# Two decoder layers on one core: first loads in order of use, one reader per PSUM bank, the last feature tile late in its group, and a fixed TensorE order in the last dilated pair

## The chip, the core and the metric

The kernel runs on 1 core of one Trainium2 chip. The metric is the device time of one execution in microseconds; three runs of the kernel before the change gave 2347.19, 2353.07 and 2353.18, so their median is 2353.07. Besides, one execution was profiled, and every row of the profile comes from that one.

## What is computed

One sequence of 512 tokens of width 1024 goes through two layers. Each layer has three sub-layers: a SwiGLU feed-forward (FFN), a token mixer and a second FFN. The mixer of layer 0 is multi-head latent attention (MLA), that of layer 1 is a dilated sliding-window attention with three dilations. Every sub-layer is wrapped in the same way:

```python
def sandwich(x, fn, pre_g, post_g, shift, scale, gate, res_w):
    hn = rmsnorm(x, pre_g) * (1 + scale[:, None, :]) + shift[:, None, :]
    y = rmsnorm(fn(hn), post_g)
    return x + res_w * gate[:, None, :] * y

def swiglu(h, w_gate, w_up, w_down):
    return (jax.nn.silu(h @ w_gate) * (h @ w_up)) @ w_down
```

Shift, scale and gate are products of silu(c) with a large matrix, `w_mod`: 2 x 1024 x 9216. All data is float32.

## The kernel before

**Layout.** Tokens are cut into four tiles of 128 (`TT`), the model width into eight tiles k of 128 (`KT`), the hidden width 2816 of an FFN into 22 feature tiles. The normed and modulated input of a sub-layer is kept transposed in `t.h`, one tile of 128 x 512 for each k.

**Three products for one.** Each float32 operand is split into a high part (`hi`, rounded to the fast matmul type) and a low part (`lo`, the rest). `mm3` (lines 123 to 128) adds hi x hi, hi x lo and lo x hi into one PSUM bank, on lines 125, 126 and 127. So every block of weights is loaded into a raw buffer (`load`, a ring of `RAW` = 5 buffers of 512 KB), copied to `whi` on ScalarE (L108) and subtracted into `wlo` on VectorE (L110). The split weights live in a ring of 6 slots (`weights`), or in general slices of 128 x 512 (`weights_sliced`, L119 and L120), of which there are 44.

**Modulation.** `mod` (L140) loads 512 KB of `w_mod` and reduces it with silu(c) on VectorE (L144). 144 such reductions are needed, 8 for each of the three vectors of each of six sub-layers. 16 are done in `start` (in halves, `mod_load` L152 and `mod_halves` L159, called `fetch` and `fold` there); the other 128 stand in the list `todo`, and `pump(n)` does the next n of them. When the last of a gate vector is done, `mod_out` writes the vector of 1024 to DRAM (`row`, L199), and `gates` reads it back broadcast (L215). `settle` pumps what a sub-layer still lacks when a border comes.

**The start.** `__init__` issues the loads of x and c and computes silu(c) on ScalarE (L71). `start` (L308) squares each token tile and sums it (L284), takes the root on GpSimd (L292), scales the tile on ScalarE (L306), transposes it on TensorE (L333) into eight banks, and then modulates k by k. The first four units (feature tiles of gate and up, `START`) are accumulated over k together, in eight banks.

**Modulating.** `modulate` (L269) makes the high part of `h` on ScalarE from the source (L275). The low part comes from a second pass over the source: on VectorE (L280, L281), or, with `spare`, on ScalarE and GpSimd (L277, L278). At a border, `turn` (L420) does this for 256 tokens with k in `SPARE` on GpSimd; the source is a PSUM bank that holds two k.

**An FFN.** Feature tiles are taken in four groups of 5 or 6 (`GROUPS`). For each, `head` multiplies gate and up (48 matmuls of 512 columns), and `gate_up_out` makes g: SiLU (L478), product (L480), high part (L481), low part (L483). After a group, `down` (L490) multiplies the group's g with its rows of `w_down`, for four token tiles i and two halves d of the width, and `y_part` adds the bank to y. The last group's `down` is `tail`, part of the border. `rest` (L515) holds the loops, and in them the calls of `pump`.

**A border.** `transition` (L390) runs `tail(i)` for the four token tiles, finishes each in `tile_done` (residual and, in `normal`, the next norm), emits `turn` for two tiles after some matmuls, and then the heads of the next sub-layer in two halves of 256 tokens.

**The dilated mixer.** Heads come in eight pairs. For each pair `scores` multiplies q and k and takes maxima, `tops` sends the maxima through DRAM to bring three dilations to one order (L1002 to L1022), `exps` does the exponentials on ScalarE (L1037), and `mix` transposes them (L1086) and multiplies with v (L1111). `Mixer.part` is the product of the first three pairs' outputs with the output weights, which is independent of the last pairs; `put_o` splits a pair's output (L599, L600).

**Order.** The framework plans the order of instructions on each engine and of the loads on SyncE's queue (SP) from the order of the program, priorities and its own estimate of when things are ready; on the chip each engine then works strictly in that order.

Of the kernel before, what the change touches and what calls it, by code (L numbers as in the profile page):

```python
# [11 lines left out]
PSUM = bass.MemoryType.PSUM  # L12

# [11 lines left out]
PUMP = 1  # L25
# [7 lines left out]
SPARE = (1, 3, 5, 7)  # L33
# [19 lines left out]
class Trunk:  # L53
    def __init__(self, ctx, tc, a):
# [16 lines left out]
        nc.scalar.activation(self.cs, self.cs, AF.Silu)  # L71
# [197 lines left out]
    def modulate(self, sub, k, lo, hi, src, spare=False):  # L269

        nc = self.nc
        a, b = self.scale(sub, k)
        u = self.t("u", UB)[:, : hi - lo]
        hh, hl = [x[k][:, lo:hi] for x in self.h]
        nc.scalar.activation(hh, src, AF.Identity, bias=b, scale=a)  # L275
        if spare:
            nc.scalar.activation(u, src, AF.Identity, bias=b, scale=a)  # L277
            nc.gpsimd.tensor_tensor(hl, u, f(hh), ALU.subtract)  # L278
        else:
            nc.vector.tensor_scalar(u, src, a, b, ALU.mult, ALU.add)  # L280
            nc.vector.tensor_tensor(hl, u, f(hh), ALU.subtract)  # L281
# [15 lines left out]

    def normal(self, i, out):

        nc = self.nc  # L300
        ss = self.pair()
        for d in range(2):
            self.square(self.x[:, i, d * SEQ : (d + 1) * SEQ], out[d], ss[:, d : d + 1])
        r = self.scale_of(ss)
        for d in range(2):
            nc.scalar.activation(out[d], self.x[:, i, d * SEQ : (d + 1) * SEQ], AF.Copy, scale=r)  # L306

    def start(self, sub):  # L308
# [18 lines left out]
        fetch(1)  # L327
        xt = [self.bank("mm" if k < 4 else "aux") for k in range(KT)]
        for i in range(TT):
            t = [self.s(), self.s()]  # L330
            self.normal(i, t)
            for k in range(KT):
                nc.tensor.transpose(  # L333
                    xt[k][:, i * P : (i + 1) * P], t[k // 4][:, k % 4 * P :][:, :P], self.ident
                )
            if i < 2:
                fold(i)
        self.new_h()
        for k in range(2):
            self.modulate(sub, k, 0, SEQ, xt[k])  # L340
        for k in range(2, KT):
            src, xt[k] = xt[k], self.s()
            if k % 2:
                nc.vector.tensor_copy(xt[k], src)
            else:
                nc.scalar.activation(xt[k], src, AF.Copy)
        units = range(START)
        banks = {}
        for u in units:
            banks[u] = [self.bank("mm" if 2 * u + g < 4 else "aux") for g in range(2)]  # L350
        for u in units:
            if u == START - 1:
                fetch(2)
            sub.gate_up_load(u, u >= SLOTS // 2)
            if u == 1:
                feed((0, 1), (0,))
                feed((0, 1), (1,))
            elif u:
                feed((u,), (0, 1))
        fold(2)  # L360
        for k in range(2, KT):
            if k + 1 < KT:
                fetch(k + 1)
            self.modulate(sub, k, 0, SEQ, xt[k])
            if k + 1 < KT:
                fold(k + 1)
            feed(units, (k,))
# [6 lines left out]
    def y_part(self, i, d, b, first):  # L374

        nc = self.nc
        with self.tc.high_priority(offset=HOT):
            y = self.y[i][d]
            if first:
                nc.scalar.activation(y, b, AF.Copy)  # L380
            else:
                nc.vector.tensor_tensor(y, b, y, ALU.add)  # L382
# [7 lines left out]
    def transition(self, sub, nxt):  # L390
# [45 lines left out]
class Ffn:  # L436
# [14 lines left out]

    def gate_up_mm(self, ft, lo, hi, banks, ks):
# [37 lines left out]
    def down(self, q, i, d):  # L490
# [8 lines left out]
        b = t.bank()  # L499
        for j in range(m):  # L500
            t.mm3(
                b,
                [x[j][:, i * P : (i + 1) * P] for x in self.g[q]],
                [x[:, d * SEQ : (d + 1) * SEQ] for x in self.wd[q][j]],
# [775 lines left out]
```

## Time and profile before

| | |
|---|---|
| three runs | 2347.19, 2353.07, 2353.18 us |
| profiled execution | 2343.64 us |
| its span | 2341.8 us |
| matmuls recorded | 11418 |
| TensorE clock granted, mean | 0.992 |
| moved by DMA | 284.55 MB, 122 GB/s in the mean |

In a row of the timeline stand the start and the duration in us, the engine, the line, the operation, what it writes and reads, how many are merged and, in brackets, how long the engine was idle before it and what released it. A row of the list of waits has the total in us, the number and the longest. A row of a window has its width, the busy time of the engines (with counts), TensorE's clock, the DMA engines' share and GB/s; where only TensorE was asked for, one busy time stands there. PE is TensorE, DVE VectorE, ACT ScalarE, POOL GpSimd, SP the queue of loads.

### The profile page before, as it was taken

What the parts mean: (1) busy time and instruction counts of PE and PEld (TensorE: products, weight loads), DVE (VectorE), ACT (ScalarE), POOL (GpSimd) and SP (SyncE); (2) the same over time, 40 slices, a digit from 0 to 9 for tenths busy, and PEclk for the clock granted to TensorE, in tenths of its full rate; (3) what the DMA queues carried; (4) which work ended last, traced back from release to release, by engine and by line L of the source; (5) the groups of instructions that cost most, each with busy time, mean ns of one, the idle gap of its engine ahead of it and who ended that gap; (6) DMA issues with size and microseconds to landing.
All of it is one profiled execution on the core that took longest, in us unless ns stands there. A gap on an engine that the chain in (4) does not pass through costs nothing. (4 is left out here: it accounts for less than half of the span.)

```text
span 2341.8 us, 30216 instructions
## 1 busy us (share of the span) xinstructions
PE 2259.5 (96%) x11418; PEld 1858.3 (79%) x11418; DVE 1182.7 (51%) x2647; ACT 890.0 (38%) x1791; POOL 116.7 (5%) x160
## 2 busy tenths in 40 slices
PE   6999999999999999999999999999999899999998
PEld 4888787877788788887888888778777668888887
DVE  6666655577564465465454453434443446333344
ACT  4332135577543132362222253443434246332222
POOL 0000001210110000030000020000000002000000
PEclk9999999999999999999999999999999999999999
DMA  8567641211264364245643523333333322233230
GB/s 307 178 211 232 206 153 62 92 55 55 67 199 140 116 198 144 72 128 170 179 140 119 163 81 102 85 94 86 89 82 90 94 54 81 91 117 99 81 108 36
DMA packets 119925, 284.55 MB, mean 122 GB/s; under 512 B 43985, under 2 KB 48356, under 8 KB 119780
## 3 DMA queue, kind: packets, MB, share of 16 engines
q1 hardware_dynamic: 119780, 282.63, 39.0%
q8 instruction: 89, 1.46, 0.2%
q14 instruction: 56, 0.46, 0.1%
HBM read 280.19 MB, written 2.39 MB: 121 GB/s over the span
## 5 line engine op out<-in xcount | busy, mean ns | idle before, releaser
L125 PE MATMUL mm<-s,whi 128*128 128x512 f32 (+1 forms) x2292 | 850.4, 373 | 8.5 <-ACT s L275 4.3
L126 PE MATMUL mm<-s,whi 128*128 128x512 f32 (+1 forms) x2292 | 846.4, 370 | 12.0 <-POOL s L278 9.8
L127 PE MATMUL mm<-s,wlo 128*128 128x512 f32 (+1 forms) x2292 | 845.1, 369 | 4.2 <-DVE wlo L110 4.2
L108 ACT ACTIVATE whi<-raw 128x1024 fp32r<-128x1024 f32 (+1 forms) x366 | 380.6, 1053 | 1016.6 <-PE mm L126 475.3
L110 DVE TENSOR_TENSOR wlo<-raw,whi 128x512 fp32r<-128x512 f32 (+1 forms) x732 | 479.2, 693 | 430.6 <-ACT whi L108 425.4
L125 PEld LDWEIGHTS mm<-s,whi 128*128 128x128 f32 x2292 | 433.4, 190 | 93.8 <-issue 7.0
L126 PEld LDWEIGHTS mm<-s,whi 128*128 128x128 f32 x2292 | 434.7, 190 | 85.4 <-POOL s L278 13.3
L127 PEld LDWEIGHTS mm<-s,wlo 128*128 128x128 f32 x2292 | 434.7, 190 | 77.2 <-DVE wlo L110 5.5
L125 PE MATMUL mm<-whi,s 128*128 128x512 f32 x848 | 333.3, 393 | 8.8 <-ACT s L481 8.7
L127 PE MATMUL mm<-whi,s 128*128 128x512 f32 x848 | 330.8, 391 | 3.5 <-DVE s L483 3.4
L126 PE MATMUL mm<-wlo,s 128*128 128x512 f32 x848 | 330.5, 390 | 0.0
L144 DVE CUSTOM_DVE_ANT_0 raw<-raw,cs 128x1024 f32<-128x1024 f32 x128 | 156.9, 1228 | 116.8 <-DMA raw<-w_mod 116.3
L125 PEld LDWEIGHTS mm<-whi,s 128*128 128x128 f32 x848 | 159.5, 188 | 45.4 <-ACT s L481 11.3
L127 PEld LDWEIGHTS mm<-whi,s 128*128 128x128 f32 x848 | 159.3, 188 | 40.2 <-DVE s L483 6.6
L126 PEld LDWEIGHTS mm<-wlo,s 128*128 128x128 f32 x848 | 159.6, 188 | 32.5 <-issue 0.2
L382 DVE TENSOR_TENSOR s<-mm,s 128x512 f32<-128x512 f32 x112 | 77.1, 689 | 163.1 <-PE mm L127 163.0
L480 DVE TENSOR_TENSOR gg<-silu,mm 128x512 f32<-128x512 f32 (+1 forms) x95 | 60.4, 636 | 161.1 <-PE mm L127 155.6
L292 POOL TENSOR_TENSOR mv<-mv,mhalf 128x1 f32<-128x1 f32 x48 | 38.1, 794 | 1590.6 <-DVE mv L291 1590.6
L481 ACT ACTIVATE s<-gg 128x512 fp32r<-128x512 f32 (+1 forms) x97 | 57.4, 592 | 62.7 <-DVE gg L480 59.4
L380 ACT ACTIVATE s<-mm 128x512 f32<-128x512 f32 x48 | 28.0, 593 | 84.2 <-PE mm L127 84.2
L1037 ACT ACTIVATE u<-u,y 128x128 f32<-128x128 f32 x128 | 49.5, 388 | 27.4 <-DVE y L1018 27.4
L937 ACT ACTIVATE s<-mm 128x512 f32<-128x512 f32 (+3 forms) x156 | 46.3, 374 | 30.7 <-PE mm L127 30.7
(159 smaller groups left out, 1485.1 us busy)
## 6 DMA issues: line engine op xcount, KB each, us to landing
raw<-w_gu SPq DMA_DIRECT2D x176, 512.0 KB, 4.6
raw<-w_mod SPq DMA_DIRECT2D x128, 512.0 KB, 4.6
raw<-w_down SPq DMA_DIRECT2D x88, 512.0 KB, 3.7
raw<-dil_in SPq DMA_DIRECT2D x72, 512.0 KB, 3.6
s<-w_mod SPq DMA_DIRECT2D x32, 256.0 KB, 6.3
raw<-mla_o SPq DMA_DIRECT2D x8, 512.0 KB, 3.5
raw<-dil_o SPq DMA_DIRECT2D x8, 512.0 KB, 4.4
gb<-row SPq DMA_DIRECT2D x6, 512.0 KB, 4.8
```

Of the source, the lines that this page charges most:

```text
L108: self.nc.scalar.activation(hi, raw, AF.Copy)
L110: self.nc.vector.tensor_tensor(lo[:, r], raw[:, r], f(hi[:, r]), ALU.subtract)
L125: mm(out, w[0], m[0], start=first, stop=False)
L126: mm(out, w[0], m[1], start=False, stop=False)
L127: mm(out, w[1], m[0], start=False, stop=last)
L144: nc.vector.tensor_tensor_reduce(raw, raw, self.cs, 1.0, 0.0, ALU.mult, ALU.add, accum_out=t[:, 0:1])
L292: nc.gpsimd.tensor_tensor(v[:, 1:2], v[:, 0:1], self.mhalf[:, 0:1], ALU.pow)
L382: nc.vector.tensor_tensor(y, b, y, ALU.add)
L480: nc.vector.tensor_tensor(v, s, banks[1], ALU.mult)
L481: nc.scalar.activation(ghi, v, AF.Copy)
L937: nc.scalar.activation(out, src, AF.Copy)
L1037: nc.scalar.activation(c, c, AF.Exp, bias=pair["top"][:, g, i, one], scale=-1.0, accum_out=pair["z"][:, g, i, one],)
```

## The change

1. Loads of the start: silu(c) moves behind the squares of x on ScalarE; the scalings go to VectorE; the work by k and by unit is interleaved (k=0, unit 0, k=1, unit 1, ...), and loads on SP keep the order of the program there.
2. `modulate` without `spare` reads its source once, on VectorE, and ScalarE makes the high part from that copy; with `spare` ScalarE alone reads it. `SPARE` becomes (2, 3, 6, 7), so that both k of a bank have the same reader. `normal` scales one half on VectorE.
3. `down` runs both halves d of token tile 0 without the last feature tile, then that one.
4. Reductions are pumped in gate and up alone: three for a unit in the first FFN, two in the others; none in `down`.
5. `prepare` loads and splits the next sub-layer's first weights into slices behind token tile 1 of a border.
6. Last dilated pair: three outputs are split and the first output weights loaded earlier, the parts' copies go to VectorE, and TensorE keeps the program's order through the parts and the mixing steps.

```diff
-PUMP = 1
-SPARE = (1, 3, 5, 7)
+SPARE = (2, 3, 6, 7)
...
         nc.sync.dma_start(self.cs, a["c"].broadcast_to([P, D]))
-        nc.scalar.activation(self.cs, self.cs, AF.Silu)
...
         hh, hl = [x[k][:, lo:hi] for x in self.h]
-        nc.scalar.activation(hh, src, AF.Identity, bias=b, scale=a)
         if spare:
+            nc.scalar.activation(hh, src, AF.Identity, bias=b, scale=a)
             nc.scalar.activation(u, src, AF.Identity, bias=b, scale=a)
             nc.gpsimd.tensor_tensor(hl, u, f(hh), ALU.subtract)
         else:
             nc.vector.tensor_scalar(u, src, a, b, ALU.mult, ALU.add)
+            nc.scalar.activation(hh, u, AF.Copy)
             nc.vector.tensor_tensor(hl, u, f(hh), ALU.subtract)
...
-        for d in range(2):
-            nc.scalar.activation(out[d], self.x[:, i, d * SEQ : (d + 1) * SEQ], AF.Copy, scale=r)
+        self.nc.scalar.activation(out[0], x[0], AF.Copy, scale=r)
+        self.nc.vector.tensor_scalar(out[1], x[1], r, None, ALU.mult)
...
         fetch(0)
-        fetch(1)
         xt = [self.bank("mm" if k < 4 else "aux") for k in range(KT)]
+        with self.tc.manual_schedule(engines={ACT, DVE}):
+            for i in range(TT):
+                t, ss, x = [self.s(), self.s()], self.pair(), self.halves(i)
+                for d in range(2):
+                    self.square(x[d], t[d], ss[:, d : d + 1])
+                r = self.scale_of(ss)
+                for d in range(2):
+                    nc.vector.tensor_scalar(t[d], x[d], r, None, ALU.mult)
+                for k in range(KT):
+                    nc.tensor.transpose(
+                        xt[k][:, i * P : (i + 1) * P], t[k // 4][:, k % 4 * P :][:, :P], self.ident
+                    )
+            nc.scalar.activation(self.cs, self.cs, AF.Silu)
         self.new_h()
...
+        for kind, n in sorted([(n, 1) for n in range(START)] + [(n, 0) for n in range(KT)]):
+            kind, n = n, kind
+            if kind:
+                sub.gate_up_load(n, n >= SLOTS // 2)
+                banks[n] = [self.bank("mm" if 2 * n + g < 4 else "aux") for g in range(2)]
+                units.append(n)
+                feed((n,), ks)
+                continue
+            if n:
+                fetch(n)
+            fold(n)
+            self.modulate(sub, n, 0, SEQ, xt[n], n in (3, 5, 7))
+            ks.append(n)
+            feed(units, (n,))
+            if n == 0:
+                for k in range(1, KT):
+                    src, xt[k] = xt[k], self.s()
+                    nc.scalar.activation(xt[k], src, AF.Copy)
...
-    def y_part(self, i, d, b, first):
+    def y_part(self, i, d, b, first, busy=False):
...
+            if not first:
+                nc.vector.tensor_tensor(y, b, y, ALU.add)
+            elif busy:
+                nc.vector.tensor_copy(y, b)
+            else:
                 nc.scalar.activation(y, b, AF.Copy)
...
                 self.after(TURN, lambda i=i: self.turn(nxt, i - 1))
+            if nxt and i == 1:
+                nxt.prepare()
...
+    def prepare(self):
+        self.gate_up_load(0, True)
...
+        b = [None, None]
+        for js in (range(m - 1), (m - 1,)) if i == 0 else (range(m),):
+            for d in range(2):
+                b[d] = b[d] or t.bank()
+                self.products(b[d], q, i, d, js)
+                if m - 1 in js:
+                    t.y_part(i, d, b[d], q == 0)
+                    if q == len(GROUPS) - 1:
+                        t.y_done(i, d)
...
                 self.head(ft, 0, SEQ)
-                t.pump(PUMP)
+                t.pump(3 if t.first is self else 2)
             for i in range(TT if q < last else 0):
-                for d in range(2):
-                    self.down(q, i, d)
-                    if t.first is self:
-                        t.pump(2 - d)
-                    elif d or q == 0:
-                        t.pump(1)
+                self.down(q, i)
...
+    def prepare(self):
+        self.w = {u: self.t.weights_sliced(self.t.a["mla_in"][u]) for u in range(2)}
...
+                if (c, i) == (7, 0):
+                    self.t.new_y()
...
+    def prepare(self):
+        t = self.t
+        self.wt = {(0, u): t.weights_sliced(t.a["dil_in"][0, u]) for u in self.ORDER[:2]}
...
         self.scores(7, 1)
+        for x in self.of[:PART]:
+            self.put_o(x)
         self.mix(6, 3)
+        t.new_y()
+        for j in range(PART):
+            self.out_weights(j)
         self.scores(7, 2)
         self.mix(6, 4)
         self.scores(7, 3)
-        for x in self.of:
+        for x in self.of[PART:]:
             self.put_o(x)
         self.exps(7)
-        for n in range(6):
-            self.part(n)
-        for step in range(5):
-            self.mix(7, step)
-            if step in (1, 2):
-                self.part(5 + step)
+        with t.tc.manual_schedule(engines={PE}):
+            for n in range(6):
+                self.part(n)
+            for step in range(5):
+                self.mix(7, step)
+                if step in (1, 2):
+                    self.part(5 + step)
         self.put_o(self.of[-1])
...
-        t.start(first)
+        with tc.manual_schedule(engines={SP}):
+            t.start(first)
```

More of the change, by code (lines that the diff above doesn't have):

```diff
@@ L12 @@
 PSUM = bass.MemoryType.PSUM
+PE, ACT, DVE, SP = (getattr(mybir.EngineType, n) for n in ("PE", "Activation", "DVE", "SP"))
 P = 128
@@ L296, in pair, with halves @@
         return self.tmp.tile([P, 2], F32, tag="ss", name="ss", bufs=6)
+    def halves(self, i):
+        return [self.x[:, i, d * SEQ : (d + 1) * SEQ] for d in range(2)]
     def normal(self, i, out):
-        nc = self.nc
-        ss = self.pair()
+        ss, x = self.pair(), self.halves(i)
         for d in range(2):
-            self.square(self.x[:, i, d * SEQ : (d + 1) * SEQ], out[d], ss[:, d : d + 1])
+            self.square(x[d], out[d], ss[:, d : d + 1])
         r = self.scale_of(ss)
-        for d in range(2):
-            nc.scalar.activation(out[d], self.x[:, i, d * SEQ : (d + 1) * SEQ], AF.Copy, scale=r)
+        self.nc.scalar.activation(out[0], x[0], AF.Copy, scale=r)
+        self.nc.vector.tensor_scalar(out[1], x[1], r, None, ALU.mult)
     def start(self, sub):
@@ L326, in start @@
         fetch(0)
-        fetch(1)
         xt = [self.bank("mm" if k < 4 else "aux") for k in range(KT)]
[L329 to L337, printed above, removed]
-        self.new_h()
-        for k in range(2):
-            self.modulate(sub, k, 0, SEQ, xt[k])
@@ L341, in start @@
[L341 to L347, printed above, removed]
-        banks = {}
[L349 to L367, printed above, removed]
+        with self.tc.manual_schedule(engines={ACT, DVE}):
[11 more added lines that the diff above has]
+            nc.scalar.activation(self.cs, self.cs, AF.Silu)
@@ L488, in head, with products, down @@
         self.gate_up_out(ft, lo, hi, banks)
-    def down(self, q, i, d):
+    def products(self, b, q, i, d, js):
+        m = GROUPS[q][1]
+        for j in js:
+            self.t.mm3(
+                b,
+                [x[j][:, i * P : (i + 1) * P] for x in self.g[q]],
+                [x[:, d * SEQ : (d + 1) * SEQ] for x in self.wd[q][j]],
+                j == 0,
+                j == m - 1,
+            )
+    def down(self, q, i):
         t = self.t
@@ L498, in down @@
                 t.new_y()
[L499 to L504, printed above, removed]
-                j == 0,
-                j == m - 1,
-            )
-        t.y_part(i, d, b, q == 0)
+        b = [None, None]
[7 more added lines that the diff above has]
+                        t.y_done(i, d)
     def tail(self, i):
-        for d in range(2):
-            self.down(len(GROUPS) - 1, i, d)
-            self.t.y_done(i, d)
+        self.down(len(GROUPS) - 1, i)
     def rest(self):
@@ L557, in __init__, with out_weights @@
         self.o = [[], []]
+    def out_weights(self, j):
+        t = self.t
+        if j not in self.wo:
+            self.wo[j] = t.weights(t.a[self.w_o][j], flat=True)
     def products(self, b, i, d, js):
@@ L574, in part @@
         i, d = divmod(n, 2)
-        if n == 0:
-            self.t.new_y()
         b = self.t.bank()
         self.products(b, i, d, range(PART))
-        self.t.y_part(i, d, b, True)
+        self.t.y_part(i, d, b, True, self.busy)
     def tail(self, i):
@@ L606 @@
     heads = 6
+    busy = False
     w_o = "mla_o"
@@ L613, in head @@
             if u == 0:
-                self.w, self.lat, self.sq = {}, {}, {}
+                self.lat, self.sq = {}, {}
                 self.latn = {}
@@ L618, in head @@
                     nc.sync.dma_start(x, t.a["mla_tab"][q])
-            self.w[u] = t.weights(t.a["mla_in"][u])
+            if u not in self.w:
+                self.w[u] = t.weights(t.a["mla_in"][u])
             self.lat[u] = t.s()
@@ L832 @@
     heads = 6
+    busy = True
     w_o = "dil_o"
```

13 lines of the change are left out of this document (5 added, 8 removed).

## The prediction

> **What bounds the kernel now.** I read the page first, then the list of who waited for whom on PE, then windows over the stages, then the timeline of each place that the list names.
>
> ```profile
> span 2341.8 us, 30216 instructions
> PE 2259.5 (96%) x11418; PEld 1858.3 (79%) x11418; DVE 1182.7 (51%) x2647; ACT 890.0 (38%) x1791; POOL 116.7 (5%) x160
> PE mm L333 <- ACT s L306: 19.5, 4, 17.0
> PE aux L1086 <- ACT sq L1037: 13.8, 5, 7.9
> PE mm L126 <- POOL s L278: 9.8, 12, 2.2
> PE mm L125 <- ACT s L481: 8.7, 5, 3.6
> PE mm L127 <- DVE s L483: 3.4, 4, 1.3
> ```
>
> TensorE is the bound: it is busy for 96% of the span, and the change takes no matmul away. All that can be won lies in the 82 us in which PE is idle, and in slow matmuls behind a stall. The rows (us in total, times, longest) name the places: the start (L333), the softmax of the dilated pairs (L1086), the hidden tiles at a sub-layer's border (L278), and the last feature tile of a group (L481, L483). The profiled execution took 2343.64 us, 1.8 more than its span; the median of the three runs shown is 2353.07, 9.4 above it. Gains are summed against the profiled one.
>
> **The start.** Now: first tokens, then weights.
>
> ```profile
> 9.98 1.06 ACT L71 ACTIVATE cs<-cs 128x1024 f32<-128x1024 f32 x1 [7.97 <-DMA cs<-c]
> 27.56 0.79 PE L125 MATMUL mm<-s,whi 128*128 128x512 f32 x1 [0.22 <-DVE u L280]
> 79.00 0.39 PE L127 MATMUL aux<-s 128*128 128x512 f32 x1
> 79.22 0.39 PE L125 MATMUL mm<-s,whi 128*128 128x512 f32 x1
> x<-x SPq DMA_DIRECT2D x4, 512.0 KB, 4.4
> 16.00:20.00 4.00, 2.20 (x9) 1.80 (x10) 1.71 (x8) 3.56 (x8) 0.71 (x2) 1.00 1.03 410
> 54.17 0.69 DVE L159 CUSTOM_DVE_ANT_0 s<-s,cs 128x512 f32<-128x512 f32 x1
> 57.49 0.15 DVE L189 SCALAR_TENSOR_TENSOR mA<-mt,small 128x1 f32<-128x1 f32 x1
> 33.07 4.30 DVE L110 TENSOR_TENSOR wlo<-raw,whi 128x512 fp32r<-128x512 f32 x7
> L280 DVE TENSOR_SCALAR u<-s,mA,mS 128x512 f32<-128x512 f32 x6 | 3.3, 546 | 0.1
> ```
>
> ACT's first operation is SiLU of c, so the squares of x, which lands earlier, stand behind it until 11. The first four units are 4 x 8 x 6 = 192 matmuls; at 0.227 us apart (79.00 to 79.22) they are 43.5 us, but they run from 27.56 to 79.22, where unit 4 begins: 8.2 us are lost after a late begin.
>
> After the change x goes first, and SP's order is k=0, unit 0, k=1, unit 1, and so on. Up to unit 0 that is 2.1 MB of x, 0.5 of c and 2.1 of weights: 4.7 MB at the 410 GB/s of the window, 11.5 us, some 15 with the launch. From then on each k with its unit is 2.1 MB, 5.1 us. DVE is slower: between 54.17 and 57.49 lie five reductions with their small operations, 0.69 each, so a fold of four is 2.8; a weight half is 4.30/7 = 0.61, a unit 2.5; modulating is 0.55 + 0.61 = 1.2. That is 6.5 us per k and unit. From about 12, when the folds can begin, DVE has k=0 and unit 0 at 19, then 25.5, 32, 37 (k=3 is modulated on ACT and POOL), and the last k near 51. PE has 6, 18, 30, 42 and four times 24 matmuls in these steps. With the first 24 at the half pace shown below it ends at 33, 40, 49.5 and 71.3. **Gain 7.5 us.** Bounds: if PE ran without a break from 18 it would end at 61.5 (gain 17.7); if the half pace and DVE's steps lasted longer, nothing is gained. The subtraction of a whole k on POOL has no row here (256 columns take 0.72, below), so 0.7 to 3.6; PE's backlog of 5.4 us per k hides it. Two orders become fixed. On ACT, SiLU of c stands behind all squares, and DVE's folds wait for it; it is 1.06 us, and ends near 12, before the first modulation weights matter to PE. On SP, the sixth 512 KB load (the second half of unit 2) waits for one of five buffers, which unit 0's split frees by 19, and the loads of k=3 stand behind it; DVE wants them at 32, so the 13 us between cover the wait and four loads of 0.65.
>
> **The last feature tile of a group.** Down products of token tile 0 need g of a unit that has just ended.
>
> ```profile
> 1074.99 1.23 DVE L144 CUSTOM_DVE_ANT_0 raw<-raw,cs 128x1024 f32<-128x1024 f32 x1 [3.09 <-DMA raw<-w_mod]
> 1076.15 0.68 DVE L480 TENSOR_TENSOR gg<-silu,mm 128x512 f32<-128x512 f32 x1
> 1077.55 0.80 PE L125 MATMUL mm<-whi,s 128*128 128x512 f32 x1 [3.62 <-ACT s L481]
> ```
>
> PE covers 12 or 15 matmuls of d=0 (2.7 or 3.4 us), then stands; here gg stood behind a modulation reduction that waited 3.09 us for its load. The change does both d without the last j first: 24 or 30 matmuls, 5.4 or 6.8 us. The cover grows by 2.7 to 3.4, and no stall of this kind is longer than 3.62. Of 8.7 + 3.4 = 12.1 us some 1 stays. Moving the reductions from down to gate-up (3 a unit in the first FFN, 2 later) puts more of them ahead of gg, so I take **11 us** of bounds 6 to 13 (matmuls right after the longest stall are slow too, as after the one below).
>
> **The sixth dilated pair, by the moved reductions.**
>
> ```profile
> 1850.15 0.38 SPq L199 DMA_DIRECT2D row<-mG  x1
> 1851.72 0.37 SPq L1015 DMA_DIRECT2D x<-m  x1
> 1864.46 0.17 DVE L1017 TENSOR_TENSOR y<-x 128x8 f32<-128x8 f32 x1 [11.52 <-DMA x<-m]
> 1869.43 1.18 PE L1086 MATMUL aux<-ident,sq 128*128 128x128 f32 x3 [7.86 <-ACT sq L1037]
> 1872.40 0.78 PE L125 MATMUL mm<-s,whi 128*128 128x512 f32 x1
> 1875.85 0.39 PE L127 MATMUL mm<-s,wlo 128*128 128x512 f32 x1
> 1910.90 0.17 DVE L1017 TENSOR_TENSOR y<-x 128x8 f32<-128x8 f32 x1 [2.23 <-DMA x<-m]
> row<-mG SPq DMA_DIRECT2D x1, 4.0 KB, 9.1
> ```
>
> The maxima come back 12.7 us after their issue; in the next pair DVE waits 2.23 for the same load. Just ahead of it in the queue stands row<-mG, 4 KB that took 9.1 us at another place, where its landing is shown. That row belongs to the last FFN: 128 reductions remain after the start, and before the change the FFNs pump 54 + 35 + 35, with 2 more at the border behind MLA, so 2 are left for the dilated layer. After it they pump 54 + 2 + 38 + 34, and all are done in the FFN ahead. The row leaves this queue. Then the maxima are in some 9 us earlier and the transposes can begin near 1860, when PE comes to them at 1861.6. Eight transposes follow; the 7.86 and 0.7 us of stall go, and the eight matmuls from 1872.40 to 1875.85, 0.43 apart, run at full pace (1.6). **Gain 11 us**, bounds 0 (another cause) to 11.6. Where the row now goes, an FFN with loads far ahead, a late weight could cost up to those 9; the row of 9.1 lay in an FFN without a stall of PE, so I take nothing.
>
> **The last pair, with PE's order fixed.**
>
> ```profile
> 1900.00:1926.00 26.00, 21.73 (x148) 15.15 (x145) 13.96 (x51) 12.98 (x54) 0.00 (x0) 0.87 0.14 23
> 1915.24 2.06 PE L1086 MATMUL aux<-ident,sq 128*128 128x128 f32 x6 [4.04 <-ACT sq L1037]
> 1921.12 0.38 ACT L1037 ACTIVATE u<-u,y 128x128 f32<-128x128 f32 x1
> ```
>
> PE runs four parts, then stands 4.04 us. The order puts six parts (54 matmuls, 12.2 us) ahead of the transposes and one between each of the next steps. That fills the stall, but ACT's exponentials still end at 1921.5, and in a fixed order PE waits there for tiles that it could pass before. I take **3 us** of bounds -2 to 5. The six copies out of PSUM go to DVE, 0.69 each as any 512-wide operation there: 4.1 more beside 13.96 of 26 us. The early weights and put_o of three tiles only fill idle time; new_y moved in MLA costs nothing.
>
> **The borders.** Five windows, width against PE's busy time:
>
> ```profile
> 399.00:425.00 26.00, 22.20 (x160) 0.93 0.46 162
> 625.00:650.00 25.00, 19.85 (x134) 1.00 0.46 148
> 1000.00:1026.00 26.00, 21.56 (x143) 1.00 0.43 130
> 1380.00:1400.00 20.00, 16.83 (x99) 0.91 0.42 139
> 1960.00:1982.00 22.00, 18.49 (x112) 0.92 0.40 141
> 1015.90 3.61 POOL L292 TENSOR_TENSOR mv<-mv,mhalf 128x1 f32<-128x1 f32 x1 [3.02 <-DVE mv L291]
> 1019.49 0.72 POOL L278 TENSOR_TENSOR s<-u,s 128x256 fp32r<-128x256 f32 x1
> 1016.02 3.09 DVE L110 TENSOR_TENSOR wlo<-raw,whi 128x512 fp32r<-128x512 f32 x5
> ```
>
> Idle: 3.8 + 5.2 + 4.4 + 3.2 + 3.5 = 20.1 us. The change splits the next weights two token tiles early (up to 2 to 4 ACT and 4 DVE operations leave the border), gives DVE one of two scalings in normal, and moves POOL from k=1 to k=2, so that the first two tiles come from DVE. ACT and DVE no longer hand a bank to each other, but hh now waits for u. The count on POOL stays four per turn. I take **8 us** of bounds 0 to 14. POOL's power at 1015.90 took 3.61 us exactly while DVE ran five splits, and the hl behind it held PE 2.2 us. The Trainium skill (SBUF — State Buffer, "Who interferes with whom") says that the pair of ports that DVE and GpSimd share is an exclusive lock, and the loser blocks; the 3.61 agrees. By that rule early splits help here, but two POOL tiles in a row, 2 and 3, double what one blocked operation holds up, and the borders would gain nothing.
>
> **Sum.** 7.5 + 11 + 11 + 3 + 8 = 40.5: 2343.64 - 40.5 = 2303 as profiled, 2312 beside the median.
>
> **Rivals.**
> - *New waits for old* at borders and group ends: POOL's pairs stall behind DVE's runs, and reductions delay gg. Borders 0, groups 6: 13 us less, 2325. For it: 3.61 and 3.09 above. Chance 0.16.
> - *The maxima are late for another cause*, such as the 512 KB load between row and maxima: 2323. Against it: other pairs have such loads too. Chance 0.08.
> - *The start stays at half pace*: PE is fed in bursts of 6 and 12. The 0.43 us above follow a stall of 7.86. The gain of 7.5 goes: 2320. The Trainium skill (TensorE: Matmul & The Clock Gate, "HAM oscillation — how this bites in real kernels") says that waits over some 3.4 us between short bursts send the clock back to half each time. Chance 0.08.
> - *Slower: DVE becomes the bound in the first FFN.*
>
> ```profile
> L144 DVE CUSTOM_DVE_ANT_0 raw<-raw,cs 128x1024 f32<-128x1024 f32 x128 | 156.9, 1228 | 116.8 <-DMA raw<-w_mod 116.3
> ```
>
> A unit is 48 matmuls, 10.9 us. DVE would have 2.5 of splits, 1.3 of g and three reductions of 1.23 with small operations, 4.5: 8.3. The row has 116.3 us of waiting for loads in 128, 0.9 each, 2.7 a unit: 11.0, just the bound. If a unit waited 6 us more, 18 units would lose over 60 with the 40 won: 2370. It decides against the change from 2.4 us a unit on. Against it: those waits fall mostly where DVE has nothing else. Chance 0.05.
> - *Nothing moves*, since the planner had these orders already: 2350. Against it: the orders on SP and PE are forced. Chance 0.03.
>
> **How the numbers follow.** The forecast has 0.60, with a range of its own of 2296 to 2322 (start 0 to 17.7, pair -2 to 5, borders to 14). The range takes in the first three rivals with some spread: 2292 to 2336. About 0.3% (7 us) is what a measurement can tell from no change, so faster means under 2346: 0.88 with the tail of the first rivals left out; within 0.06; slower 0.06.
>
> **What would show it.** PE's first matmul near 19 and unit 4 near 71; no row<-mG in the dilated layer and no wait for x<-m over 3 us; L481 and L483 gone from PE's list; L1086 under 5 us; the five border windows with some 12 us of idle. It is wrong if DVE waits for w_mod in gate-up show behind PE stalls for weight splits, or if POOL's waits grow.

## The result, and the profile after

Four runs of the changed kernel gave 2309.79 to 2314.05 us, median **2313.09**; four of the kernel before in the same group gave 2344.48 to 2353.18, median 2350.13. The ratio is 0.9843, with a 95% interval of [0.9818, 0.9867]. The forecast was 2312. The changed kernel's profiled execution took 2314.05 us, 29.6 less than the 2343.64 of before, where 40.5 had been summed: between the medians lie 37.0, and the profiled execution of before lay below all four runs of its kernel, that of after is the slowest of its four. The sum of the steps is therefore judged against the 29.5 us by which the two profiled spans differ, the stages against each other. One run of the kernel before, in the last group of experiments, took 6388.67 us and is left out everywhere.

The page, first part, of the kernel after:

```profile
span 2312.3 us, 30176 instructions
...
PE 2247.3 (97%) x11418; PEld 1857.3 (80%) x11418; DVE 1191.8 (52%) x2674; ACT 870.6 (38%) x1773; POOL 121.4 (5%) x163
```

The list of what PE waited for, of the kernel after (us in total, times, longest):

```profile
PE mm L124 <- DVE s L378: 16.4, 1, 16.4
PE mm L125 <- POOL s L277: 14.5, 13, 2.2
PE mm L124 <- ACT s L280: 7.6, 4, 6.4
PE mm L339 <- DVE s L337: 7.1, 1, 7.1
PE aux L248 <- POOL rs L242: 2.6, 4, 1.2
PE aux L1107 <- ACT sq L1058: 1.7, 4, 0.9
```

The lines have moved: L339 is the transposes of the start (L333 before), L280 the high part of h, L277 GpSimd's subtraction (L278), L1107 the transposes of a dilated pair (L1086), L378 the copy of a part out of PSUM, which is new on VectorE. Read against the list of before: the start's 19.5 us became 7.1 + 7.0 (of L280's), the group ends (L481 and L483, 12.1) are gone, the pairs' 13.8 became 1.7. Two rows speak against the forecast. GpSimd's wait rose from 9.8 to 14.5, which the prediction had named as a sign of being wrong, and one stall of 16.4 us is new, longer than anything that was removed behind the start.

Stage by stage, from PE's timeline (a border is counted from its first transpose on L427 to its last, a body from one border to the next; the last body ends with the last matmul, and the last dilated pair begins with the first matmul of its parts, at 1902.40 before and 1863.10 after):

| stage | before | after | gain | forecast |
|---|---|---|---|---|
| start, to unit 4 | 79.2 | 71.4 | 7.8 | 7.5 |
| four FFN bodies (the first from unit 4) | 1364.9 | 1345.6 | 19.3 | 11 |
| MLA body | 201.0 | 201.7 | -0.7 | 0 |
| five borders | 134.1 | 130.7 | 3.4 | 8 |
| dilated layer, through pair 6 | 500.3 | 489.7 | 10.6 | 11 |
| its last pair and parts | 54.0 | 64.9 | -10.9 | 3 |

These add up to 29.5.

### The profile page after: what moved, and what is told of

It reads as the page before. It is cut to its first block, busy times and chain, and to the rows that moved or that the text cites. A ratio compares the mean times of both kernels' runs of the same rounds, so it can differ in the third digit from the quotient of the medians.

```text
span 2312.3 us, 30176 instructions
## 1 busy us (share of the span) xinstructions
PE 2247.3 (97%) x11418; PEld 1857.3 (80%) x11418; DVE 1191.8 (52%) x2674; ACT 870.6 (38%) x1773; POOL 121.4 (5%) x163
## 5 line engine op out<-in xcount | busy, mean ns | idle before, releaser
L124 PE MATMUL mm<-s,whi 128*128 128x512 f32 (+1 forms) x2132 | 804.7, 379 | 10.2 <-ACT s L280 7.0
L125 PE MATMUL mm<-s,whi 128*128 128x512 f32 (+1 forms) x2132 | 800.2, 375 | 0.9 <-POOL s L277 0.7
L126 PE MATMUL mm<-s,wlo 128*128 128x512 f32 (+1 forms) x2132 | 799.1, 375 | 0.0
L107 ACT ACTIVATE whi<-raw 128x1024 fp32r<-128x1024 f32 (+1 forms) x356 | 370.2, 1053 | 989.8 <-PE mm L125 447.8
L109 DVE TENSOR_TENSOR wlo<-raw,whi 128x512 fp32r<-128x512 f32 (+1 forms) x712 | 464.9, 692 | 414.2 <-ACT whi L107 409.2
L124 PEld LDWEIGHTS mm<-s,whi 128*128 128x128 f32 x2132 | 403.6, 190 | 92.7 <-ACT s L280 8.2
L125 PEld LDWEIGHTS mm<-s,whi 128*128 128x128 f32 x2132 | 403.9, 189 | 71.7 <-POOL s L277 2.1
L126 PEld LDWEIGHTS mm<-s,wlo 128*128 128x128 f32 x2132 | 403.8, 189 | 71.2
L124 PE MATMUL mm<-whi,s 128*128 128x512 f32 x848 | 333.4, 393 | 17.1 <-DVE s L378 16.4
L483 DVE TENSOR_TENSOR gg<-silu,mm 128x512 f32<-128x512 f32 (+1 forms) x95 | 60.3, 636 | 172.4 <-PE mm L126 172.0
L292 POOL TENSOR_TENSOR mv<-mv,mhalf 128x1 f32<-128x1 f32 x48 | 27.3, 568 | 1492.6 <-DVE mv L291 1492.6
L481 ACT ACTIVATE silu<-mm 128x512 f32<-128x512 f32 (+1 forms) x95 | 51.6, 544 | 34.0 <-PE mm L126 33.7
L125 PE MATMUL mm<-s 128*128 128x256 f32 x160 | 47.6, 303 | 14.8 <-POOL s L277 13.8
```

Of the source, the lines that this page charges most:

```text
L107: self.nc.scalar.activation(hi, raw, AF.Copy)
L109: self.nc.vector.tensor_tensor(lo[:, r], raw[:, r], f(hi[:, r]), ALU.subtract)
L124: mm(out, w[0], m[0], start=first, stop=False)
L125: mm(out, w[0], m[1], start=False, stop=False)
L126: mm(out, w[1], m[0], start=False, stop=last)
L292: nc.gpsimd.tensor_tensor(v[:, 1:2], v[:, 0:1], self.mhalf[:, 0:1], ALU.pow)
```

## The experiments

Each kernel is the changed one with one edit, unless it says otherwise; times are medians of four runs, beside runs of the kernel before on the same chip. There were four groups: `parts_first` to `down_whole`; `spare_old` to `prepare_off`; the changed kernel again with `silu_first` and `pf_sub`; and `pumps_back`. The kernel before took 2351.9, 2344.8, 2346.4 and 2348.5 us in them, so between groups the ratios are compared. Line numbers shift by one where an edit adds or takes a line.

| kernel | us | ratio to before |
|---|---|---|
| changed kernel, with the result above | 2313.09 | 0.9843 [0.9818, 0.9867] |
| changed kernel, again (third group) | 2312.03 | 0.9855 [0.984, 0.987] |
| `parts_first` | 2300.86 | 0.9786 [0.9765, 0.9808] |
| `free_order` | 2303.65 | 0.9798 [0.9779, 0.9818] |
| `row_back` | 2321.9 | 0.9881 [0.9858, 0.9904] |
| `down_whole` | 2320.79 | 0.987 [0.9848, 0.9892] |
| `spare_old` | 2304.9 | 0.983 [0.9816, 0.9845] |
| `sub_dve` | 2297.58 | 0.9798 [0.9783, 0.9813] |
| `sp_free` | 2319.17 | 0.9893 [0.9876, 0.9909] |
| `prepare_off` | 2315.49 | 0.9876 [0.9859, 0.9893] |
| `silu_first` | 2314.22 | 0.9866 [0.985, 0.9883] |
| `pumps_back` | 2328.3 | 0.991 [0.9894, 0.9927] |
| `pf_sub` (two edits) | 2286.43 | 0.9743 [0.9729, 0.9758] |

### The new stall in the last pair

VectorE's timeline of the kernel after, around the stall:

```profile
1871.44 0.17 DVE L1038 TENSOR_TENSOR y<-x 128x8 f32<-128x8 f32 x1 [2.94 <-DMA x<-m]
...
1886.65 0.17 DVE L1079 TENSOR_TENSOR w<-x 128x8 f32<-128x8 f32 x1 [14.84 <-DMA x<-z]
...
1887.26 2.43 DVE L378 COPY s<-mm 128x512 f32<-128x512 f32 x4
```

L1079 is the denominators of the softmax on their way back from DRAM: they exist only when all exponentials are done, so VectorE stands 14.84 us. The four copies, whose sources PE had finished by 1871.5, lie behind it in the same queue, back to back as soon as it lets go. PE has four banks for parts, all full, and its fixed order forbids it to go on to anything else. In `parts_first` the parts are emitted ahead of the exponentials, so that the copies stand ahead of L1079; in `free_order` the copies stay behind it and PE's order is free.

```diff
 parts_first:
-        self.exps(7)
         with t.tc.manual_schedule(engines={PE}):
             for n in range(6):
                 self.part(n)
+            self.exps(7)
 free_order:
-        with t.tc.manual_schedule(engines={PE}):
-            for n in range(6):
+        for n in range(6):
...
```

> The six parts are emitted ahead of the exponentials of the last dilated pair; all else as in the changed kernel. Theory (VectorE's queue): the 16.4 us stall of PE came because the copies of the parts' banks stood on VectorE behind the sum of the softmax denominators, which waits for a round trip through DRAM. Then the stall goes, PE waits some 2 us for the first exponentials instead, and the kernel takes some 11 to 14 us less than the changed one: a profiled execution near 2301. Rival (TensorE's fixed order alone): the stall stays near 16 us, at the same place, and the time stays near 2313.

> The fixed TensorE order of the last dilated pair is taken away; all else as in the changed kernel. Theory (VectorE's queue and the fixed order together): the copies of the banks still stand behind the denominators, but PE may run the transposes meanwhile, so that the stall falls to that of the kernel before, 3 to 6 us, and the time by some 9 to 12 us to 2302. Rival (VectorE's queue alone, the order adds nothing): the stall stays over 12 us and the time near 2313.

VectorE's timeline of `parts_first`:

```profile
1863.46 1.88 DVE L378 COPY s<-mm 128x512 f32<-128x512 f32 x3
...
1867.24 0.16 DVE L1038 TENSOR_TENSOR y<-x 128x8 f32<-128x8 f32 x1
...
1868.67 0.69 DVE L378 COPY s<-mm 128x512 f32<-128x512 f32 x1 [1.07 <-PE mm L126]
...
1870.71 0.69 DVE L378 COPY s<-mm 128x512 f32<-128x512 f32 x1 [1.35 <-PE mm L126]
...
1886.33 0.17 DVE L1079 TENSOR_TENSOR w<-x 128x8 f32<-128x8 f32 x1
```

L1079 is as late as in the kernel after, at 1886.33, and PE does not stand for it, since the copies that it needs are done. From the fourth border's end to the fifth's begin it is 541.0 us (1369.1 to 1910.1) instead of 554.6: 13.6 less, and the ratios say 13 to 16. PE's timeline of `free_order`:

```profile
1874.04 1.18 PE L1107 MATMUL aux<-ident,sq 128*128 128x128 f32 x3 [4.36 <-ACT sq L1058]
```

Here PE goes on to other tiles; the 4.36 us are of the kind and the size that the kernel before had (4.04). So neither the fixed order nor the move to VectorE does the harm alone: a copy behind a wait for DRAM is harmless to a PE that may pass it, and a fixed order is harmless where nothing that it waits for stands behind such a wait. The fixed order with the copies back on ScalarE was not tried.

### The row and the sixth pair

```diff
-                t.pump(3 if t.first is self else 2)
+                t.pump(min(3 if t.first is self else 2, max(0, len(t.todo) - 2)))
```

Two reductions are left over and fall into the dilated layer, as they did before; all else stays.

> Two of the 128 reductions are kept back for the dilated layer, as in the kernel before; all else as in the changed kernel. Theory (the 4 KB row of the last gate vector blocks the queue): a load of the maxima again comes back some 10 us late, PE stands 6 to 9 us at a transpose of that pair, and the time rises by 8 to 11 us to some 2323. Rival (another cause, such as the 512 KB load between them): no pair's maxima are late and the time stays near 2313.

The row is back on SP's queue at 1816.36. VectorE's timeline of `row_back`:

```profile
1831.33 0.17 DVE L1038 TENSOR_TENSOR y<-x 128x8 f32<-128x8 f32 x1 [11.94 <-DMA x<-m]
```

And PE's:

```profile
1836.31 0.97 PE L1107 MATMUL aux<-ident,sq 128*128 128x128 f32 x2 [8.28 <-ACT sq L1058]
```

The two rows of before are there again (11.52 and 7.86). From the fourth border to the fifth it takes 565.9 us instead of 554.6, 11.3 more; the term was 11. The whole takes only 6.7 us more by the spans and 6 to 9 by the ratios, since three of its borders are shorter by 4.2 in all (the two causes of that are shown with `silu_first`, below). With the row came the 512 KB load behind it (1816.80), which no other pair has between its maxima. That such a load alone does not make them late is seen at a denominators' trip, in the timeline of SP's queue of the kernel after:

```profile
1778.74 0.36 SPq L99 DMA_DIRECT2D raw<-dil_in  x1
1779.63 0.38 SPq L1076 DMA_DIRECT2D x<-z  x1
...
1783.51 0.37 SPq L1082 DMA_DIRECT2D d<-w  x1
```

w is made from x on VectorE, so x, issued 0.9 us behind a load, was back in less than 3.9 us. And the load behind the row was late itself: in `row_back` the row took 11.5 us to land and that load 14.3, where the median of such loads (raw<-dil_o) is 3.7 in the kernel after. The rival "late for another cause" has little left; row and load were not tried apart.

### Group ends: the late feature tile and the moved reductions

`down_whole` takes the late last feature tile back and leaves the reductions where the change put them; `pumps_back` does the opposite.

```diff
 down_whole:
-        for js in (range(m - 1), (m - 1,)) if i == 0 else (range(m),):
+        for js in (range(m),):
 pumps_back:
-                t.pump(3 if t.first is self else 2)
+                t.pump(1)
             for i in range(TT if q < last else 0):
                 self.down(q, i)
+                t.pump(3 if t.first is self else 2 if q == 0 else 1)
```

> Token tile 0 takes its feature tiles in one piece, as in the kernel before; pumping stays as in the changed kernel. Theory (the cover by the other half of the width removed the stalls): PE waits again for g at the ends of groups, 8 to 16 us in total, with the reductions now all in gate and up, and the time rises by 9 to 18 us to 2322 to 2331. Rival (moving the reductions out of down removed them): the waits stay under 4 us and the time under 2317.

> The reductions are pumped as before the change, one for a unit of gate and up and the rest behind each token tile of down; the late last feature tile and all else stay. With it two reductions and the row go back to the dilated layer, which costs 8 to 11 us there by the run that did that alone. Theory (the move out of down gave the feed-forward bodies the 8 us that the late feature tile does not explain): the two middle bodies take 3 to 5 us longer each, and the time is 2328 to 2334 us. Rival (where the reductions stand is of no matter to the bodies): they stay within 1 us of 342.8 and 344.3, and the time is 2320 to 2325 us.

What PE waited for, of `down_whole`:

```profile
PE mm L126 <- DVE s L486: 4.8, 7, 1.1
...
PE mm L124 <- ACT s L484: 2.1, 2, 1.4
```

And of `pumps_back`, in the body between its third and fourth borders (1004 to 1356 us):

```profile
PE mm L124 <- ACT s L484: 1.4, 1, 1.4
PE mm L126 <- DVE s L486: 0.4, 1, 0.4
```

Both expectations were partly off. Without the late tile 6.9 us of waits return, not 8 to 16, none longer than 1.4, and the first three bodies take 10.0 us more (2.7 + 3.5 + 3.8). The whole takes 8.1 us more by the spans and only 4 to 6 by the ratios: its fourth border is 1.5 shorter. With the reductions back in `down`, the three take 4.6 more (0.5 + 1.7 + 2.4), between theory and rival; the rest of the 13.6 us in its span is mostly the row, which returned to the dilated layer (10.4). In neither kernel does the long stall of before (3.62, gg behind a reduction that waited for its load) return: each of the two edits alone takes it away. If the two add, 14.6 of the 19.3 us are so assigned. Of the other 4.7, some 1.0 lie in the last body, which neither edit changed; the rest, that stall among it, is not assigned.

Note the rate: 6.9 us of listed waits cost 10.0 us of these bodies. The clock is not the reason, since it is 1.00 through all three. In PE's timeline of `down_whole` matmuls begin 0.23 us apart while each is recorded as 0.39 long, so that the list begins to count late: at one stall they begin at 686.21 and 687.69, 1.25 more than 0.23 apart, and 1.09 is listed; the next one follows after 0.33. That is some 0.3 us for each of nine stalls.

### The borders

```diff
 spare_old:
-SPARE = (2, 3, 6, 7)
+SPARE = (1, 3, 5, 7)
 sub_dve:
-            nc.gpsimd.tensor_tensor(hl, u, f(hh), ALU.subtract)
+            nc.vector.tensor_tensor(hl, u, f(hh), ALU.subtract)
 prepare_off:
-            if nxt and i == 1:
-                nxt.prepare()
+            if nxt and i == 1 and not isinstance(nxt, Ffn):
+                nxt.w, nxt.wt = {}, {}
```

> Only the list of spare tiles goes back to (1, 3, 5, 7), so that no two of GpSimd's subtractions follow each other at a border. Theory (the border's remaining stall is GpSimd's second subtraction in a row, 14.5 us over 13 waits with one of 1.3 to 2.2 us at each of the five borders): the long waits go, L277's mean falls from 1179 ns towards the 896 ns that it had before, and some 6 to 10 us come off: 2303 to 2307 us. Rival (the list only says which tile is late; VectorE and ScalarE are as busy as before): waits of the old kind return, L275, wlo or L281 among them, and the time is 2310 to 2316 us.

> GpSimd's subtractions at the borders and at the start go to VectorE; nothing else changes. Theory (GpSimd is what the border waits for): its 14.5 us of waits go, VectorE takes on eight subtractions of some 0.4 us at each border, 3 us beside 20 of 27 busy, and the time is 2302 to 2309 us. Rival (a border is bound by VectorE's queue, and GpSimd was only the last in line): waits for L281 and for wlo come in the same places, and the time is 2311 to 2320 us.

> The early loads of the next layer's first weights at a border are taken out: each layer loads and splits its first weights where its first unit begins, as before. Theory (the early loads are what removed the waits for wlo and whi at the borders, 4.2 and 0.8 us in the five border windows before): those waits return, 3 to 6 us: 2316 to 2319 us, and GpSimd's second subtraction in a row stays at 2 us or more. Rival (the early splits, which fall on VectorE and ScalarE in the border itself, are what holds GpSimd's pairs up): L277's waits fall under 8 us and the time stays at 2308 to 2314 us.

Windows over the five borders, of the kernel after (from and to, width, then busy us and counts of PE, PEld, DVE, ACT, POOL, the granted clock, the DMA engines' share, GB/s):

```profile
379.00:408.00 29.00, 25.70 (x178) 23.22 (x177) 20.92 (x42) 18.44 (x41) 8.98 (x9) 1.00 0.41 141
609.00:636.00 27.00, 22.38 (x154) 19.73 (x153) 21.79 (x42) 19.52 (x41) 9.11 (x9) 1.00 0.40 130
977.00:1004.00 27.00, 24.15 (x151) 21.81 (x150) 19.75 (x38) 18.69 (x40) 9.00 (x9) 0.94 0.31 98
1347.00:1374.00 27.00, 24.15 (x152) 21.83 (x151) 20.15 (x39) 18.83 (x40) 8.26 (x8) 0.94 0.36 116
1928.00:1954.00 26.00, 22.63 (x148) 20.32 (x147) 19.68 (x38) 18.51 (x40) 9.35 (x9) 0.93 0.37 122
```

17.0 us of idle are left (136.0 less 119.0), where 12 had been forecast. The third border, GpSimd's timeline of the kernel after:

```profile
989.27 0.73 POOL L277 TENSOR_TENSOR s<-u,s 128x256 fp32r<-128x256 f32 x1 [1.12 <-ACT u L276]
...
993.30 4.33 POOL L277 TENSOR_TENSOR s<-u,s 128x256 fp32r<-128x256 f32 x2 [2.27 <-ACT u L276]
```

One subtraction alone took 0.73 us; the two that are merged in the last row took 4.33. Taken apart, the first ran from 993.30 to 996.42, 3.12 us, and the second until 997.63; PE, which had stopped at 994.0, began again at 996.47, with the end of the first. VectorE's timeline of the same kernel at that place:

```profile
993.33 0.69 DVE L109 TENSOR_TENSOR wlo<-raw,whi 128x512 fp32r<-128x512 f32 x1
993.93 0.69 DVE L414 TENSOR_TENSOR x<-x,s 128x512 f32<-128x512 f32 x1
994.53 1.29 DVE L109 TENSOR_TENSOR wlo<-raw,whi 128x512 fp32r<-128x512 f32 x2
995.74 0.70 DVE L291 SCALAR_TENSOR_TENSOR mv<-ss 128x1 f32<-128x1 f32 x1
996.36 0.68 DVE L109 TENSOR_TENSOR wlo<-raw,whi 128x512 fp32r<-128x512 f32 x1
```

VectorE had been in a run of operations with two inputs in SBUF since 991.73 and went on with it without a gap; its next one began 0.03 us after GpSimd's. The subtraction ended not with the run but with L291, at 996.42 and 996.44: a sum of 128x1, which took 0.70 us here and 0.15 to 0.18 at 43 of its 48 places. So GpSimd seems to have been shut out by the operations of 128x512 and let in at the small one, which then waited for it. Each of the five borders has one such subtraction, of 3.1 to 3.8 us, each ends within 0.03 us of an L291 of some 0.7, and none of before was over 1.73. The prediction named the rule for it and what the sum would be by it, "the borders would gain nothing" (the Trainium skill, SBUF — State Buffer, "Who interferes with whom": the loser of the ports that VectorE and GpSimd share is blocked). The trace agrees with the block, 3.12 us; not with "two POOL tiles in a row" as the way, since it is the first of the two that is long. With the old list the durations of L277 in `spare_old` (lowest, median, highest) are:

```profile
L277 POOL TENSOR_TENSOR s<-u,s x43: 723/742/1803, 39.0 to 1950.4; 128x256 fp32r<-128x256 f32 x40, 128x512 fp32r<-128x512 f32 x3
```

and in the kernel after:

```profile
L277 POOL TENSOR_TENSOR s<-u,s x43: 725/744/3818, 38.9 to 1958.9; 128x256 fp32r<-128x256 f32 x40, 128x512 fp32r<-128x512 f32 x3
```

The long ones are gone with the list. How is not settled. In `spare_old` a subtraction that began at 993.32, within a run of four splits on VectorE (992.48 to 995.51), took 1.04 us, and one of the splits took 1.23 instead of 0.68, so a run does not always shut GpSimd out. Nor does the new list always bring five of them: `parts_first` and `silu_first` have three.

What PE waited for, of `spare_old`:

```profile
PE mm L125 <- POOL s L277: 6.7, 11, 0.9
PE mm L124 <- ACT s L275: 3.3, 5, 1.4
```

14.5 became 6.7, L275 rose by 2.4, and the five borders take 120.8 us instead of 130.7. The span is 8.9 us shorter; by the ratios it is 3 to 6 us, with intervals that touch those of the changed kernel, so the direction is the profile's and the size is open. The old list mixes two readers in a bank, so of "one reader per PSUM bank" no gain is to be seen: what the new list costs on GpSimd is more.

`sub_dve` takes GpSimd out. Groups by line and form, of `sub_dve`:

```profile
L277 DVE TENSOR_TENSOR s<-u,s 128x256 fp32r<-128x256 f32 x40 | 17.3, 433 | 2.3 <-ACT u L276 2.2
...
L281 DVE TENSOR_TENSOR s<-u,s 128x256 fp32r<-128x256 f32 x40 | 16.4, 420 | 2.3 <-ACT s L280 2.3
```

And of the kernel after, where L281's mean is 476 ns:

```profile
L277 POOL TENSOR_TENSOR s<-u,s 128x256 fp32r<-128x256 f32 x40 | 46.8, 1179 | 55.0 <-ACT u L276 51.4 <-PE mm L126 3.3
```

1179 ns became 433, and VectorE's own subtractions (L281) went from 476 ns to 420. The borders take 116.4 us, 14.3 less, and the ratios 0.9798 against 0.9843 and 0.9855 leave no overlap: some 10 to 13 us. That was more than the 4 to 11 expected.

`prepare_off` settled little. Neither side came true: PE's list shows no wait for wlo or whi in a border, so the early loads are not what removed those, and L277's waits did not fall but rose.

```profile
PE mm L125 <- POOL s L277: 17.4, 13, 2.7
```

(The row is from the list of what PE waited for, of `prepare_off`.) Its borders take 132.0 us, 1.3 more; by the time it can't be told from the changed kernel. What took away the waits for wlo is open.

### The start

```diff
 sp_free:
-        with tc.manual_schedule(engines={SP}):
-            t.start(first)
+        t.start(first)
 silu_first:
         nc.sync.dma_start(self.cs, a["c"].broadcast_to([P, D]))
+        nc.scalar.activation(self.cs, self.cs, AF.Silu)
...
-            nc.scalar.activation(self.cs, self.cs, AF.Silu)
```

> SP's written order around the start is taken away, so that the planner's order stands there: nine gate-and-up blocks of 512 KB go ahead of the second block of w_mod, instead of two at a time between them; x ahead of c stays. Theory (the order of the loads carries most of the start's 7.8 us): the modulation of the second tile waits for its block of w_mod behind some 3.5 MB, and the fourth gate-and-up unit begins 5 to 15 us later than at 71.4: 2318 to 2328 us. Rival (x ahead of c carries it, and the other loads fit beside each other in any order): 2311 to 2315 us.

> The activation Silu of c goes back to the head of ScalarE's queue, ahead of the squares of x; the loads' order and all else stay. Theory (ScalarE's first square stood behind Silu's wait for c until 10.95 where it now begins at 4.35, and the start gains by it): the transposes begin some 6 us later, and the first matmul of the feed-forward network 3 to 6 us later than 19.48, the time 3 to 6 us above the changed kernel's. Rival (the first matmul waits for w_mod and its addition, not for x): the transposes move and the first matmul stays within 1 us, the time within 2 us.

PE's timeline of `sp_free`:

```profile
21.94 1.27 PE L124 MATMUL mm<-s,whi 128*128 128x512 f32 x2 [8.36 <-ACT s L280]
...
35.16 0.79 PE L124 MATMUL mm<-s,whi 128*128 128x512 f32 x1 [6.84 <-ACT s L280]
```

The first FFN matmul is 2.5 us later than in the kernel after (19.48), and a second stall of 6.84 follows; unit 4 begins at 80.8 instead of 71.4, and the first border at 388.9 instead of 379.4. The written order of the loads is worth 9.5 us there; for the whole the ratios say 9 to 12. PE's timeline of `silu_first`:

```profile
15.10 1.12 PE L340 MATMUL mm<-ident,s 128*128 128x128 f32 x4 [15.10 <-DVE s L338]
...
23.52 0.50 PE L125 MATMUL mm<-s,whi 128*128 128x512 f32 x1 [2.49 <-ACT s L281]
```

The transposes begin 8.0 us later, the first matmul 4.0 later and the first border 4.6 later than in the kernel after: the theory's place is right. But the whole takes only 2 us more, within the intervals. Its four later borders are shorter, about 24.2 us each instead of 25.5, and there are two causes. The second and the fifth have no long subtraction. The third and the fourth have it, with the same stall of 2.2 us, but another clock. Their windows, of `silu_first`, in the columns of the borders above:

```profile
981.00:1006.00 25.00, 22.15 (x151) 19.98 (x150) 19.69 (x39) 18.96 (x41) 9.01 (x9) 1.00 0.32 106
1349.00:1374.00 25.00, 22.16 (x150) 19.91 (x149) 19.95 (x38) 18.60 (x40) 8.27 (x8) 1.00 0.33 109
```

The kernel after has 151 and 152 matmuls in windows of 27.00 us there, at a clock of 0.94. So what Silu's place cost at the start was made up further on by things that the edit did not aim at, and a gain at the start need not reach the end one to one.

### The two repairs together

> The changed kernel as it stands, beside the kernel before on the chip of this group, since the kernel before has differed between groups by 7 us (2344.78 and 2351.9). If its ratio is steady from chip to chip it comes out at 0.982 to 0.987, 2305 to 2318 us; the other two kernels of this group are read against it.

> Two edits together: the last pair's parts are emitted ahead of the last exponentials, and GpSimd's subtractions of the modulation go to VectorE. Theory (the last pair's 16.4 us stall and the borders' waits for GpSimd lie at different places on the path): the gains of the two alone add up, some 14 and 12 us against the changed kernel by their ratios: 2284 to 2290 us where the changed kernel takes 2313. Rival (with the stall gone the last border is reached with VectorE still behind, so that it gives part of it back): 2291 to 2297 us.

`pf_sub` took 2286.43 us beside 2312.03 for the changed kernel in the same group, 25.6 less, and is the fastest of all: ratio 0.9743 to the kernel before. The gains add up, within the 13 to 16 and 10 to 13 us of the two alone. At one place the rival shows: the last border takes 24.2 us, 1.4 more than in `sub_dve`. From the page of `pf_sub`:

```profile
PE 2241.7 (98%) x11418; PEld 1853.9 (81%) x11418; DVE 1196.8 (52%) x2717; ACT 869.5 (38%) x1773; POOL 72.6 (3%) x120
```

What PE waited for, of `pf_sub`, the two largest:

```profile
PE mm L124 <- ACT s L280: 7.8, 3, 6.5
PE mm L339 <- DVE s L337: 7.6, 2, 7.1
```

The long waits of both are of the start; nothing else in its list has a wait over 1.5 us.

## Why the prediction was right, and where its steps were not

- **The start**: right in place and size. First matmul at 19.48 (forecast 19), unit 4 at 71.40 (71.3). `sp_free` shows the order of the loads behind it, `silu_first` ScalarE's queue. It did not stay at half pace: the granted clock was 0.50 from 19.4 to 28.4 us and 1.00 from 28.5 to unit 4. (The prediction's own 79.2 and 71.3 give 7.9, not 7.5.)
- **Group ends**: the mechanism was right, the term "I take 11 us of bounds 6 to 13" too small: the bodies gained 19.3. The sum counted each stall by its length alone; `down_whole` shows 10.0 us of time for 6.9 of listed waits. And the moved reductions, which the step feared, helped (4.6 in `pumps_back`): they leave the place where gg stood behind them. The slower rival (VectorE bound in the first FFN) has nothing in the list.
- **The sixth pair**: right. The row, gone to the FFN ahead (issued at 1273.90), cost nothing there: no wait for a weight came with it. Two things about this step were loose. Its parts, 7.86 + 0.7 + 1.6, add to 10.2, and 11 was taken where 10.6 came. And its argument against the rival, "other pairs have such loads too", does not hold: no other pair has a load between its maxima. What speaks against the rival is `row_back`.
- **The last pair**: wrong in sign, and outside its bounds: "3 us of bounds -2 to 5" was -10.9. The step that failed is the costing of the six copies as "4.1 more beside 13.96 of 26 us". It weighed VectorE's load and not its queue: it did not ask which instruction the copies stand behind, nor how many banks PE has while they wait. It sought what PE's fixed order waits for on ScalarE, and it was VectorE.
- **The borders**: too high, 3.4 of 8 and inside the bounds. The first rival, new waits for old, was half right: at the borders GpSimd stood behind VectorE's run as it said and its waits grew, at the group ends nothing did. The step that failed is "I take 8 us" against a rule and a row (3.61) that both spoke for less.
- **The sum** came out near because the group ends' surplus of 8.3 and the last pair's shortfall of 13.9 partly cancel; 40.5 was summed, 29.5 is in the profiled executions and 34 to 37 in the medians. The base helped too: the forecast started from a median of 2353.07, and the kernel before took 2350.13 beside the result. That the time lay 1 us from the forecast is thus partly luck.

## What to carry to other kernels

When work moves to an engine that seems half idle, look up which instruction it will stand behind: a queue that waits for a trip through DRAM is closed for its whole length, whatever its share of busy time. A fixed order on the bound engine makes every such wait its own, so emit what it needs ahead of the wait, or leave it free to pass. A GpSimd operation on the path beside runs of two-input operations on VectorE took four or five times its length here; VectorE did the same subtraction faster itself.

## What the runs showed of the hardware

**A stall of 2.2 us costs more than itself, and the bill comes later.** Windows of PE alone, of the kernel after, around the third border's stall (from and to, width, PE busy, granted clock, DMA share, GB/s):

```profile
990.00:994.00 4.00, 3.94 (x33) 1.00 0.05 15
994.00:996.50 2.50, 0.30 (x4) 1.00 0.81 193
996.50:998.00 1.50, 1.50 (x12) 0.93 0.99 396
998.00:1000.00 2.00, 2.00 (x11) 0.50 0.64 252
1000.00:1002.00 2.00, 2.00 (x14) 0.70 0.83 223
```

The granted clock is 1.00 through the stall, and falls to 0.50 some 1.3 us after PE is back at work, until between 1001 and 1002: 0.1 + 1.0 + 0.6 = 1.7 us of full speed lost beside the 2.2 waited. The Trainium skill (TensorE: Matmul & The Clock Gate, "HAM oscillation — how this bites in real kernels") gives as the rule that PE should not idle for more than some 3.4 us; these rows show the drop after a shorter gap, though not each time: the first two borders had stalls of 2.2 and 2.1 us and a clock of 1.00, and the fifth had 0.93 with none over 1.3. The third and fourth borders of `silu_first` and `row_back` have the same stall of 2.2 us and 1.00; they take 24.1 us where the kernel after takes 25.6, so 1.5 us of such a border hang on the clock alone. What decides it is not shown by any run here. Three borders of the kernel before and three of the kernel after have a clock of 0.93 or 0.94, so it does not change the gain of 3.4; `sub_dve` has one, so some 3 of its 14.3 us may be the clock. This is also why the windows' idle time undercounts what such a border loses.

**What VectorE and GpSimd do to each other is lopsided**: VectorE's subtraction (L281) took 476 ns in the mean of the kernel after, 504 in `spare_old`, and 420 in `sub_dve`, where GpSimd has none; GpSimd's took 0.73 us alone and up to 3.82 beside VectorE's runs.
